# Output projection and second FFN product with the activations stationary and the weights streamed 512 wide

## The chip, the cores and the metric

The kernel runs on one core of a Trainium2 chip. The metric is the device time in microseconds; the median of three runs of the kernel before is 356.52 (356.47 to 356.79). PE is the matmul engine, ACT and DVE the two engines for elementwise work, SP the queue that issues the transfers.

## The reference, cut to what matters

One decoder block over 256 tokens of 1024 features, all in fp32. What the change touches is the end of the attention part and the FFN:

```
proj = einsum('bsd,de->bse', rms_norm(x, attn_norm_g), w_in)   # q, k, v, forget and gate logits
... two attention branches o_a, o_b of 512 features each ...
merged = gates[:, :, 0] * (o_a @ w_branch_moba) + gates[:, :, 1] * (o_b @ w_branch_fox)
x = x + einsum('bsd,de->bse', merged, w_out)                    # 1024 -> 1024
h2 = rms_norm(x, ffn_norm_g)
up = einsum('bsd,df->bsf', h2, w_ffn_up)                        # 1024 -> 2 * 2816
u, g = split(up, 2, axis=-1)
g = causal_depthwise_conv(g, ffn_conv_w, ffn_conv_b)            # 3 taps over the tokens
x = x + einsum('bsf,fd->bsd', silu(g) * u, w_ffn_down)          # 2816 -> 1024
```

## The kernel before

Every matrix product is made of fp32r matmuls on split operands: a value is the sum of a high part (rounded to fp32r by ACT) and a low part (the rest, by DVE). A product takes three terms: high x high, high x low, low x high.

**Weights.** They come in chunks of 1 MB in a fixed list (`chunks`: qkv, wg, wb, wo, then wu with wd between), over three raw buffers. Each chunk has two halves of 128 x 1024. `load` issues the transfer on SP and writes the split of a half: L125 on ACT makes `whi`, L126 on DVE makes `wlo`. There are six pairs of `whi`/`wlo` buffers (`HB`), and `use` asks for the splits five halves ahead (`AHEAD`). So a split waits until PE has read the half six places earlier.

**Layout.** The q/k/v projections (`project`, L236) hold a tile of 128 tokens stationary and stream 512 weight columns; their result is tokens by features. All products behind the attention hold 128 x 128 of weights stationary and stream 256 tokens; their result is features by tokens. So x1 (x plus the attention part, in place of `xT`), the FFN and the result stand features by tokens.

**Around the change.** `wb` (L527 to L529) makes `mh`, `ml`, the parts of merged. The output projection (L553 to L555) has four chunks: 0 and 1 cover the first half of the contraction, 2 and 3 the second. With chunks 2 and 3, each half finishes two blocks of 128 features: DVE adds the residual (L558), ACT and DVE make the parts of x1 times the norm's gain, `hx` (L562, L563; tag `pp`), and ACT squares (L564). The sums of squares go through a matmul with ones in `norm2` (L572), called in the middle of the second up tile, and become `rs2`, by which the FFN's products are scaled afterwards (L600). The first FFN product (`up_products`, L590 and L591) has 22 tiles; one matmul streams both parts of `hx` 512 wide, one the high part against the low weights. The second (`down`, L639 to L641) comes after every second up tile, in eleven steps, and accumulates into four PSUM banks; in the last step the result's blocks are finished one after another, each with an add (L619) and a store.

PE's order is written out by hand and is the program order. The order of ACT's and DVE's queues is made by a scheduler when the kernel is built; each engine works through its queue strictly in that order.

Of the kernel before, what the change touches and what calls it, by code (L numbers as in the profile page):

```python
# [8 lines left out]
F32 = mybir.dt.float32  # L9
# [32 lines left out]
def decoder_block(ctx, tc, a, out):  # L42
# [7 lines left out]
    def T(shape, tag, bufs=1, dt=F32):  # L50
        return sb.tile(shape, dt, tag=tag, bufs=bufs, name=tag)

    def bank():
        return ps.tile([P, 512], F32, tag="bank", bufs=8, name="bank")
# [395 lines left out]
    def banks():  # L450
        return [bank() for _ in range(NT)]
# [13 lines left out]
    project(2, pv, 1)  # L465
    finish_v(pv, 0)
    pq = banks()
    project(3, pq, 0)
    turn_qk(qn, kn, 0)
    project(3, pq, 1)  # L470
# [66 lines left out]


    hx = T([P, KT, 2, 2, P], "pp", 1, F32R)
    sq2 = T([P, 4, 2 * S], "V")  # L540
    acc = [bank() for _ in range(4)]
    x1 = xT
    sqs = T([P, S], "sqs")
    for c in range(4):
        for h in range(2):
            wh, wl = use(("wo", c), h)
            j = 2 * (c % 2) + h
            for i in range(2):
                o = acc[j][:, i * S:(i + 1) * S]
                for k4 in range(4):  # L550
                    k = 4 * (c // 2) + k4
                    w = slice(k4 * 256 + i * P, k4 * 256 + (i + 1) * P)
                    nc.tensor.matmul(o, wh[:, w], pairs(mh[:, k]), start=(k == 0 and i == 0), stop=False)  # L553
                    nc.tensor.matmul(o, wh[:, w], pairs(ml[:, k]), start=False, stop=False)  # L554
                    nc.tensor.matmul(o, wl[:, w], pairs(mh[:, k]), start=False, stop=(k == KT - 1 and i == 1))  # L555
            if c >= 2:
                xx = x1[:, 2 * j:2 * j + 2]
                nc.vector.tensor_tensor(halves(xx), apart(acc[j]), halves(xx), op=ALU.add)  # L558
                for b in (2 * j, 2 * j + 1):
                    g = col(C_G2 + b)  # L560
                    xb = x1[:, b].rearrange("p (a t) -> p a t", a=2)
                    nc.scalar.activation(hx[:, b, :, 0], xb, AF.Copy, scale=g)  # L562
                    nc.vector.scalar_tensor_tensor(hx[:, b, :, 1], xb, g, hx[:, b, :, 0].bitcast(F32), op0=ALU.mult, op1=ALU.subtract)  # L563
                nc.scalar.activation(sq2[:, j].rearrange("p (b t) -> p b t", b=2), xx, AF.Square)  # L564
    for dst, src in ((0, 1), (2, 3), (0, 2)):
        nc.vector.tensor_tensor(sq2[:, dst], sq2[:, dst], sq2[:, src], op=ALU.add)
    nc.vector.tensor_tensor(sqs, sq2[:, 0, 0:S], sq2[:, 0, S:2 * S], op=ALU.add)
    rs2 = T([P, S], "rs2")

    def norm2():  # L570
        sp = bank()
        nc.tensor.matmul(sp[:, 0:S], ones, sqs, start=True, stop=True)  # L572
        rsqrt_mean(rs2, sp[:, 0:S], D, [S], "pT", 4)


    acts = {}
# [1 line left out]
    def up_products(f):  # L578
        two = banks()
        for h in range(2):  # L580
            if f == 1 and h == 1:
                norm2()
            wh, wl = use(("wu", f), h)
            for i in range(2):
                for k4 in range(4):
                    k = 4 * h + k4
                    w = slice(k4 * 256 + i * P, k4 * 256 + (i + 1) * P)
                    both = hx[:, k].rearrange("p a l t -> p (l t) a")
                    high = hx[:, k, :, 0].rearrange("p a t -> p t a")
                    nc.tensor.matmul(two[i], wh[:, w], both, start=(k == 0), stop=False)  # L590
                    nc.tensor.matmul(two[i][:, 0:S], wl[:, w], high, start=False, stop=(k == KT - 1))  # L591
        return two

    def up_finish(f, two):
# [17 lines left out]
        nc.scalar.activation(ah, av, AF.Copy)  # L612
        nc.vector.tensor_tensor(al, av, ah.bitcast(F32), op=ALU.subtract)

    acc = []
    yy = lt[:, :, S:2 * S]

    def residual(dst, ps_, d, n):
        nc.vector.tensor_tensor(halves(dst), apart(ps_, n), halves(x1[:, d:d + n]), op=ALU.add)  # L619

    def down(p):
        if p == 0:
            acc[:] = [(b, c) for b in banks() + banks() for c in (0, S)]
        ac = acts.pop(p)
        last = p == NF // 2 - 1
        if last:
            acc[6:] = [(bank(), 0) for _ in range(2)]
        w2 = [use(("wd", p), h) for h in range(2)]
        order = [(h, d) for d in ((0, 1), (2, 3), (4, 5), (6,), (7,)) for h in range(2)] if last else [(h, (d,)) for h in range(2) for d in range(KT)]
        for h, ds in order:  # L630
            wh, wl = w2[h]
            ah, al = pairs(ac[:, h]), pairs(ac[:, 2 + h])
            for d in ds:
                bk, c = acc[d]
                o = bk[:, c:c + S]
                w = slice(d * P, (d + 1) * P)
                first = h == 0 and c == 0 and (p == 0 or last and d > 5)
                end = h == 1 and (d == ds[-1] if last else p == NF // 2 - 2 and d == KT - 1)
                nc.tensor.matmul(o, wh[:, w], ah, start=first, stop=False)  # L639
                nc.tensor.matmul(o, wh[:, w], al, start=False, stop=False)  # L640
                nc.tensor.matmul(o, wl[:, w], ah, start=False, stop=end)  # L641
            if last and h == 1:
                n = len(ds)
                y = yy[:, ds[0]:ds[0] + n]
                residual(y, acc[ds[0]][0][:, 0:n * S], ds[0], n)
                nc.sync.dma_start(out[:, ds[0]:ds[0] + n], y)
        if p == NF // 2 - 2:
            residual(x1[:, 6:8], acc[6][0], 6, 2)

    first = [up_products(f) for f in range(2)]  # L650
    for f in range(NF):
        up_finish(f, first[f] if f < 2 else up_products(f))
# [6 lines left out]
def _layout(i):  # L659
    f = np.float32  # L660
    x = i["x"][0]
    w = i["w_in"][0]
    k128 = lambda m: m.reshape(-1, P, m.shape[1]).transpose(1, 0, 2)
    c = np.ascontiguousarray
    a = {}
    w6 = w[:, :6 * W4].reshape(D, 6, W4 // 2, 2).transpose(0, 1, 3, 2).reshape(D, 6 * W4)
    qkv = w6.reshape(2, 4, P, 6, W4)
    a["qkv"] = c(qkv.transpose(3, 0, 2, 1, 4).reshape(6, 2, P, 2048)[1:])
    lead = np.concatenate([x.T.reshape(KT, P, S), w6[:, :W4].reshape(KT, P, W4)], 2)
    a["lead"] = c(lead)  # L670
    a["wf"] = c(k128(w[:, 6 * W4:6 * W4 + NH]))
    wg = w[:, 6 * W4 + NH:].reshape(KT, P, 2, KT, P)
    a["wg"] = c(wg.transpose(3, 1, 0, 2, 4).reshape(KT, P, 2048))
    wb = np.concatenate([i["w_branch_moba"][0], i["w_branch_fox"][0]]).reshape(KT, P, 4, 256)
    a["wb"] = c(wb.transpose(2, 1, 0, 3).reshape(4, P, 2048))
    wo = i["w_out"][0].reshape(2, 4, P, 2, 2, 256)
    a["wo"] = c(wo.transpose(0, 3, 2, 4, 1, 5).reshape(4, P, 2048))
    wu = i["w_ffn_up"][0].reshape(KT, P, 2, NF, P)
    a["wu"] = c(wu.transpose(3, 1, 0, 2, 4).reshape(NF, P, 2048))
    a["wd"] = c(i["w_ffn_down"][0].reshape(NF // 2, 2, P, D).transpose(0, 2, 1, 3).reshape(NF // 2, P, 2048))  # L680
    sm = np.empty((P, C_END), f)
    a["g1"] = c(i["attn_norm_g"][0].reshape(KT, P).T)
    sm[:, C_G2:C_G2 + 8] = i["ffn_norm_g"][0].reshape(KT, P).T
    sm[:, C_BG:C_BG + 16] = i["b_gate"][0].reshape(2 * KT, P).T
    sm[:, C_CW:C_CW + 66] = i["ffn_conv_w"][0].reshape(3 * NF, P).T
    sm[:, C_CB:C_CB + 22] = i["ffn_conv_b"][0].reshape(NF, P).T
    gm = ["moba_q_norm_g", "moba_k_norm_g", "fox_q_norm_g", "fox_k_norm_g"]
    for j, n in enumerate(gm):
        sm[0:64, C_QG + j] = sm[64:128, C_QG + j] = i[n][0]
        if j < 2:  # L690
            sm[0:16, C_QG + j] = sm[64:80, C_QG + j] = 1.0
            sm[:, C_GR + 16 * j:C_GR + 16 * (j + 1)] = i[n][0][None, 0:16]
    sm[:, C_BF:C_BF + 8] = i["b_forget"][0][None]
    a["smalls"] = sm
    cs = np.zeros((P, 832), f)
    cs[:, 0:128] = np.eye(P)
    tri = np.tril(np.ones((P, P), f))
    cs[:, 128:256] = tri.T
    cs[:, 256:384] = 1.0
    mask = np.where(tri > 0, f(0), f(BIG))  # L700
    cs[:, 384:512] = mask
    cs[:, 640:768] = mask
    inv = np.power(f(500000.0), -np.arange(HALF, dtype=f) * f(2.0) / f(16)).astype(f)
    ang = np.arange(S, dtype=f)[:, None] * inv[None]
    co, si = np.cos(ang), np.sin(ang)
    tab = np.concatenate([co, co, si, -si], 1).reshape(NT, P, 32).transpose(1, 0, 2)
    cs[:, 768:832] = tab.reshape(P, 64)
    a["consts"] = cs
    return a
# [15 lines left out]
```

## Time and profile before

| | |
|---|---|
| median of three runs | 356.52 us |
| profiled execution | 357.34 us, span 355.5 us |
| PE busy | 350.4 us, 99% |
| DVE busy | 285.5 us, 80% |
| ACT busy | 228.8 us, 64% |
| read from memory | 66.6 MB, 190 GB/s over the span |

Busy time of PE is modelled and says little; the distance between the starts of two matmuls says how fast the stream is. In the timeline a row has the start, the duration, engine, line, operation, output and inputs, stationary shape and streamed shape, and in brackets the idle time before it and what ended that. In the chain of waits a piece has its start, its length and what it was.

### The profile page before, as it was taken

Reading aid. Unit: us, or ns where it says so; the run is one execution under the profiler, and the core shown is the slowest. Engines: PE = TensorE matmul, PEld = TensorE weight load, DVE = VectorE, ACT = ScalarE, POOL = GpSimd, SP = SyncE. Lnnn points to the kernel's source line nnn. Section 1 sums busy time; section 2 is a strip of 40 time slices with the busy share of each in tenths; the row PEclk is TensorE's granted clock in tenths of the full one; section 3 lists DMA queues with packets and bytes.
Section 4 is the critical chain, followed back from the end, with each engine's and each line's share of the span. In section 5 each row is a group of like instructions: output and inputs, shape, how many; then the busy total and the mean of one; then the engine's idle time right before and its main releaser. Section 6 shows DMA issues by size and latency. Waiting matters only on the chain.

```text
span 355.5 us, 6596 instructions
## 1 busy us (share of the span) xinstructions
PE 350.4 (99%) x2620; PEld 324.3 (91%) x2620; DVE 285.5 (80%) x534; ACT 228.8 (64%) x406; POOL 0.4 (0%) x6
## 2 busy tenths in 40 slices
PE   8999999999999999999999999999999999999995
PEld 4888888889899999999999999999999999999995
DVE  4989969888867756994997998897878788797953
ACT  5967576678849873553878866665756656666620
POOL 0000000000000000000000000000000000000000
PEclk9999999999999999999999999999999999999999
DMA  7986663663624453545644358655645646554003
GB/s 259 410 336 237 221 255 130 227 237 120 238 92 147 133 225 118 202 166 227 229 144 187 153 165 295 211 193 206 236 162 194 238 166 205 223 189 167 2 0 118
DMA packets 12558, 68.07 MB, mean 191 GB/s; under 512 B 1512, under 2 KB 3696, under 8 KB 5104
## 3 DMA queue, kind: packets, MB, share of 16 engines
q1 hardware_dynamic: 11328, 66.60, 51.7%
q10 hardware_dynamic: 1200, 1.06, 1.0%
q8 instruction: 20, 0.33, 0.4%
q14 instruction: 10, 0.08, 0.1%
HBM read 66.60 MB, written 1.06 MB: 190 GB/s over the span
## 4 chain that ended last, share of the span: by engine, by line
PE 98%; ACT 1%; DVE 0%; issue 0%
PE bank L590 22%; PE bank L236 18%; PE bank L591 11%; PE bank L641 6%; PE bank L640 6%; PE bank L639 5%; PE bank L436 4%; PE bank L438 4%; PE bank L437 4%; PE bank L527 2%; PE bank L555 2%; PE bank L554 2%; PE bank L529 2%; PE bank L528 2%; PE bank L553 2%; PE bank L411 2%
## 5 line engine op out<-in xcount | busy, mean ns | idle before, releaser
L126 DVE TENSOR_TENSOR wlo<-raw,whi 128x1024 fp32r<-128x1024 f32 x118 | 144.0, 1222 | 38.2 <-ACT whi L125 37.2
L125 ACT ACTIVATE whi<-raw 128x1024 fp32r<-128x1024 f32 x118 | 123.7, 1054 | 66.5 <-PE bank L590 20.7
L590 PE MATMUL bank<-pp,whi 128*128 128x512 f32 x352 | 116.2, 383 | 0.0
L591 PE MATMUL bank<-pp,wlo 128*128 128x256 f32 x352 | 95.9, 273 | 0.0
L590 PEld LDWEIGHTS bank<-pp,whi 128*128 128x128 f32 x352 | 66.6, 189 | 9.2
L591 PEld LDWEIGHTS bank<-pp,wlo 128*128 128x128 f32 x352 | 67.6, 192 | 0.0
L436 PE MATMUL bank<-xh,whi 128*128 128x256 f32 x128 | 35.6, 278 | 0.1
L437 PE MATMUL bank<-xl,whi 128*128 128x256 f32 x128 | 35.2, 275 | 0.0
L438 PE MATMUL bank<-xh,wlo 128*128 128x256 f32 x128 | 35.2, 275 | 0.0
L639 PE MATMUL bank<-qT,whi 128*128 128x256 f32 x112 | 30.8, 275 | 0.0
L640 PE MATMUL bank<-qT,whi 128*128 128x256 f32 x112 | 30.8, 275 | 0.0
L641 PE MATMUL bank<-qT,wlo 128*128 128x256 f32 x112 | 30.8, 275 | 0.0
L236 PE MATMUL bank<-whi,xh 128*128 128x512 f32 x96 | 29.8, 393 | 0.0
L236 PE MATMUL bank<-wlo,xh 128*128 128x512 f32 x96 | 29.1, 385 | 0.0
L236 PE MATMUL bank<-whi,xl 128*128 128x512 f32 x96 | 28.7, 380 | 0.0
L436 PEld LDWEIGHTS bank<-xh,whi 128*128 128x128 f32 x128 | 24.6, 192 | 1.1 <-ACT qT L282 0.5
L438 PEld LDWEIGHTS bank<-xh,wlo 128*128 128x128 f32 x128 | 24.6, 192 | 0.0
L437 PEld LDWEIGHTS bank<-xl,whi 128*128 128x128 f32 x128 | 24.6, 192 | 0.0
L639 PEld LDWEIGHTS bank<-qT,whi 128*128 128x128 f32 x112 | 21.5, 192 | 0.2
L640 PEld LDWEIGHTS bank<-qT,whi 128*128 128x128 f32 x112 | 21.5, 192 | 0.0
L641 PEld LDWEIGHTS bank<-qT,wlo 128*128 128x128 f32 x112 | 21.5, 192 | 0.0
L236 PEld LDWEIGHTS bank<-wlo,xh 128*128 128x128 f32 x96 | 18.3, 192 | 3.1 <-DVE wlo L103 0.6
(158 smaller groups left out, 644.7 us busy)
## 6 DMA issues: line engine op xcount, KB each, us to landing
raw<-in_wu SPq DMA_DIRECT2D x22, 1024.0 KB, 4.8
raw<-in_wd SPq DMA_DIRECT2D x11, 1024.0 KB, 4.8
raw<-in_qkv SPq DMA_DIRECT2D x9, 1024.0 KB, 5.0
raw<-in_wg SPq DMA_DIRECT2D x8, 1024.0 KB, 4.9
raw<-in_wb SPq DMA_DIRECT2D x4, 1024.0 KB, 5.2
raw<-in_wo SPq DMA_DIRECT2D x4, 1024.0 KB, 4.8
lead<-in_lead SPq DMA_DIRECT2D x8, 384.0 KB, 6.6
raw<-in_qkv SPq DMA_DIRECT2D x2, 512.0 KB, 8.0
```

What stands on the lines that cost most here:

```text
L125: whi = nc.scalar.activation(hi, raw, AF.Copy)
L126: nc.vector.tensor_tensor(lo, raw, hi.bitcast(F32), op=ALU.subtract)
L236: nc.tensor.matmul(pt[t], lhs[:, k, t * P:(t + 1) * P], rhs, start=(k == 0 and i == 0), stop=(k == KT - 1 and i == 2))
L411: nc.tensor.matmul(op[o:o + HD, n * S + i * P:(n + 1) * S], V[:, i, vc:vc + HD], pT[:, j, c], start=(i == 0), stop=(i == 1))
L436: nc.tensor.matmul(o, wh[:, w], rh, start=(k == 0 and i == 0), stop=False)
L437: nc.tensor.matmul(o, wh[:, w], rl, start=False, stop=False)
L438: nc.tensor.matmul(o, wl[:, w], rh, start=False, stop=(k == KT - 1 and i == 1))
L590: nc.tensor.matmul(two[i], wh[:, w], both, start=(k == 0), stop=False)
L591: nc.tensor.matmul(two[i][:, 0:S], wl[:, w], high, start=False, stop=(k == KT - 1))
L639: nc.tensor.matmul(o, wh[:, w], ah, start=first, stop=False)
L640: nc.tensor.matmul(o, wh[:, w], al, start=False, stop=False)
L641: nc.tensor.matmul(o, wl[:, w], ah, start=False, stop=end)
```

## The change

The weights of the output projection and of the second FFN product are now streamed 512 columns at a time past stationary tiles of 128 x 128 activations, as in the q/k/v projections. x1 and the result become tokens by features. x is therefore loaded a second time, in that order (`xn`, 1 MB), over the place of `xT`. The output projection makes four tiles of 128 tokens x 512 features; each holds both halves of a weight chunk for both token tiles. The input of the first FFN product must still stand features by tokens, so x1 goes through 16 transposes on PE (`turn_x`), out of whose banks ACT and DVE make the parts of `hx` (`split_h`). The squares are summed by ACT along the features; `norm2` works on two columns and is called ahead of the first up tile, and `norm2_row` spreads its result by a matmul in the middle of the second up tile. Weights and result are rearranged on the host, outside the time.

```diff
+    x1 = xT
+    nc.sync.dma_start(x1, a["xn"])
     project(3, pq, 0)
...
-    for c in range(4):
-        for h in range(2):
-            wh, wl = use(("wo", c), h)
-            ...
-                    nc.tensor.matmul(o, wh[:, w], pairs(mh[:, k]), start=(k == 0 and i == 0), stop=False)
...
+    def wo(kh, dh, t, w2):
+        for h in range(2):
+            wh, wl = w2[h]
+            for k2 in range(2):
+                k = 4 * kh + 2 * h + k2
+                rh, rl = (pairs(w[:, k2 * 512:(k2 + 1) * 512]) for w in (wh, wl))
+                for i, (lhs, rhs) in enumerate(((mh, rh), (mh, rl), (ml, rh))):
+                    nc.tensor.matmul(acc[t][dh], lhs[:, k, t * P:(t + 1) * P], rhs, start=(k == 0 and i == 0), stop=(k == KT - 1 and i == 2))
+
+    def residual(t, dh):
+        xx = x1[:, place(t, dh)]
+        nc.vector.tensor_tensor(xx, wide(acc[t][dh]), xx, op=ALU.add)
+        nc.scalar.activation(T([P, 2, S], "sq", 2), xx, AF.Square, accum_out=ssq[:, t, dh:dh + 1])
+
+    def turn_x(dh, t):
+        for j in range(2):
+            if t == 0:
+                hb[dh, j] = bank()
+            for b in range(2):
+                c = b * S + t * P
+                nc.tensor.transpose(hb[dh, j][:, c:c + P], x1[:, 4 * t + 2 * dh + j, b * P:(b + 1) * P], ident)
+
+    def split_h(dh):
+        for j in range(2):
+            for b in range(2):
+                d = 4 * dh + 2 * j + b
+                src = hb[dh, j][:, b * S:(b + 1) * S].rearrange("p (a t) -> p a t", a=2)
+                g = col(C_G2 + d)
+                nc.scalar.activation(hx[:, d, :, 0], src, AF.Copy, scale=g)
+                nc.vector.scalar_tensor_tensor(hx[:, d, :, 1], src, g, hx[:, d, :, 0].bitcast(F32), op0=ALU.mult, op1=ALU.subtract)
+
+    for kh in range(2):
+        for dh in range(2):
+            w2 = [use(("wo", 2 * kh + dh), h) for h in range(2)]
+            for t in range(NT):
+                wo(kh, dh, t, w2)
+                if kh == 1:
+                    residual(t, dh)
+                if kh == 1 and dh == 1 and t == 0:
+                    for u in range(NT):
+                        turn_x(0, u)
+                    split_h(0)
+    turn_x(1, 0)
+
+    def last_turn():
+        turn_x(1, 1)
+        split_h(1)
...
+                if f == 0 and h == 0 and i == 0:
+                    last_turn()
...
+            for i, (lhs, rhs) in enumerate(((ah, rh), (ah, rl), (al, rh))):
+                nc.tensor.matmul(o, lhs, rhs, start=(first and i == 0), stop=(end and i == 2))
...
+            for h in range(2):
+                for dh in range(2):
+                    for t in range(NT):
+                        end = h == 1 and p == NF // 2 - 2 and t == dh == 1
+                        tile_of(h, t, dh, acc[t][dh], every, p == 0 and h == 0, end)
...
+    r2 = norm2()
     first = [up_products(f) for f in range(2)]
```

On ACT, at the seam between output projection and first up tile, the queue of the kernel before: `L562` makes a high part of `hx`, `L125` the split of a weight half, `L564` a square, `L598` belongs to the FFN.

```order
L562 ACTIVATE pp_1999<-lead_79,sm_80 128x2x128 x2
L564 ACTIVATE V_2000<-lead_79 128x512
L125 ACTIVATE whi_2269<-raw_2226 128x1024
L562 ACTIVATE pp_1999<-lead_79,sm_80 128x2x128 x2
L564 ACTIVATE V_2000<-lead_79 128x512
L125 ACTIVATE whi_2291<-raw_2289 128x1024
L598 ACTIVATE lows_2364<-bank_2267 128x256
L125 ACTIVATE whi_2313<-raw_2289 128x1024
L598 ACTIVATE lows_2364<-bank_2268 128x256
L125 ACTIVATE whi_2344<-raw_2342 128x1024
L190 ACT_TABLE_LOAD
```

The same place of ACT's queue now: `L580` makes a high part out of a bank of transposes (2140 holds blocks 0 and 1, 2143 blocks 2 and 3, 2173 blocks 4 and 5, 2176 blocks 6 and 7), `whi_2121` and `whi_2191` are the halves of chunk wu 2, `L564` the square of the last tile.

```order
L580 ACTIVATE pp_2000<-bank_2140,sm_80 128x2x128
L125 ACTIVATE whi_2121<-raw_2119 128x1024
L580 ACTIVATE pp_2000<-bank_2143,sm_80 128x2x128
L125 ACTIVATE whi_2191<-raw_2119 128x1024
L564 ACTIVATE sq_2171,ssq_2005<-lead_79 128x512
L580 ACTIVATE pp_2000<-bank_2173,sm_80 128x2x128
L580 ACTIVATE pp_2000<-bank_2176,sm_80 128x2x128
L580 ACTIVATE pp_2000<-bank_2173,sm_80 128x2x128
L190 ACT_TABLE_LOAD
L190 ACTIVATE rsv_2182<-rsv_2182 128x2
L580 ACTIVATE pp_2000<-bank_2176,sm_80 128x2x128
L191 ACT_TABLE_LOAD
```

Two splits now stand among the high parts, and the table load of the norm, which stood behind the first FFN evacuations, stands ahead of the high part of block 7; the second high part out of a bank waits for DVE's low part of the first.

On DVE, the end of the seam before: `L558` is a residual, `L563` a low part of `hx`, `L126` the low half of a weight split, `L566` an add of squares.

```order
L558 TENSOR_TENSOR lead_79<-bank_2003,lead_79 128x2x256
L126 TENSOR_TENSOR wlo_2229<-raw_2226,whi_2228 128x1024
L563 SCALAR_TENSOR_TENSOR pp_1999<-lead_79,sm_80,pp_1999 128x2x128 x2
L558 TENSOR_TENSOR lead_79<-bank_2004,lead_79 128x2x256
L126 TENSOR_TENSOR wlo_2270<-raw_2226,whi_2269 128x1024
L563 SCALAR_TENSOR_TENSOR pp_1999<-lead_79,sm_80,pp_1999 128x2x128 x2
L566 TENSOR_TENSOR V_2000<-V_2000 128x512 x2
```

And now: `L563` is a residual, `L581` a low part out of the same banks, `L603` the add of the sums of squares.

```order
L563 TENSOR_TENSOR lead_79<-bank_2002,lead_79 128x2x256
L581 SCALAR_TENSOR_TENSOR pp_2000<-bank_2140,sm_80,pp_2000 128x2x128
L581 SCALAR_TENSOR_TENSOR pp_2000<-bank_2143,sm_80,pp_2000 128x2x128
L581 SCALAR_TENSOR_TENSOR pp_2000<-bank_2140,sm_80,pp_2000 128x2x128
L126 TENSOR_TENSOR wlo_2122<-raw_2119,whi_2121 128x1024
L581 SCALAR_TENSOR_TENSOR pp_2000<-bank_2143,sm_80,pp_2000 128x2x128
L563 TENSOR_TENSOR lead_79<-bank_2004,lead_79 128x2x256
L126 TENSOR_TENSOR wlo_2192<-raw_2119,whi_2191 128x1024
L603 TENSOR_TENSOR ss2_2179<-ssq_2005 128x2
L581 SCALAR_TENSOR_TENSOR pp_2000<-bank_2173,sm_80,pp_2000 128x2x128
```

A weight split moved ahead of the low part of block 3 and of the last residual, another ahead of the low part of block 4.

## Rows read from the trace of the kernel before

**Rows 1.** The page: PE's busy time, and its granted clock in 40 slices.
```profile
PE 350.4 (99%) x2620; PEld 324.3 (91%) x2620; DVE 285.5 (80%) x534; ACT 228.8 (64%) x406; POOL 0.4 (0%) x6
...
PEclk9999999999999999999999999999999999999999
```

**Rows 2.** The page: the chain of waits by engine.
```profile
PE 98%; ACT 1%; DVE 0%; issue 0%
```

**Rows 3.** Timeline of PE: start and duration in us, 256-wide matmuls, and what follows.
```profile
155.33 0.28 PE L553 MATMUL bank<-xh,whi 128*128 128x256 f32 x1
...
176.77 0.38 PE L590 MATMUL bank<-pp,whi 128*128 128x512 f32 x1
...
340.84 0.28 PE L639 MATMUL bank<-qT,whi 128*128 128x256 f32 x1
...
346.20 0.28 PE L639 MATMUL bank<-kT,whi 128*128 128x256 f32 x1
```

**Rows 4.** Timeline of PE: first and twenty-first of a run of 512-wide matmuls.
```profile
40.72 0.59 PE L236 MATMUL bank<-wlo,xh 128*128 128x512 f32 x2
...
45.03 0.38 PE L236 MATMUL bank<-whi,xl 128*128 128x512 f32 x1
```

**Rows 5.** Chain of waits at the seam: start, length in us, what.
```profile
180.21 0.27 PE bank L590
...
180.59 0.29 PE bank L590
```

**Rows 6.** Chain of waits: fp32 passes of 128 (L423, L345) and 256 columns.
```profile
27.47 0.44 PE bank L423 x4
...
58.00 0.22 PE bank L345 x2
...
184.92 0.43 PE bank L572 x2
```

**Rows 7.** Timeline of ACT, output projection to second up tile.
```profile
166.20 1.06 ACT L125 ACTIVATE whi<-raw 128x1024 fp32r<-128x1024 f32 x1 [1.63 <-PE bank L554]
...
173.43 0.61 ACT L564 ACTIVATE V<-lead 128x512 f32<-128x512 f32 x1
...
185.97 1.28 ACT L190 ACT_TABLE_LOAD   x1
187.26 0.42 ACT L190 ACTIVATE pT<-pT 128x256 f32<-128x256 f32 x1
```

**Rows 8.** Timeline of DVE at the seam.
```profile
175.80 1.21 DVE L126 TENSOR_TENSOR wlo<-raw,whi 128x1024 fp32r<-128x1024 f32 x1
176.93 0.87 DVE L563 SCALAR_TENSOR_TENSOR pp<-lead,sm,pp 128x256 fp32r<-128x256 f32 x2
177.72 0.68 DVE L558 TENSOR_TENSOR lead<-bank,lead 128x512 f32<-128x512 f32 x1
```

**Rows 9.** Groups by line and form, whole span: busy us, mean ns | idle.
```profile
L598 ACT ACTIVATE lows<-bank 128x256 f32<-128x256 f32 x44 | 16.3, 371 | 2.1 <-PE bank L591 2.1
...
L382 ACT ACTIVATION_READ_ACCUMULATOR s<-s,nm 128x1 f32 x32 | 6.2, 192 | 0.0
...
L562 ACT ACTIVATE pp<-lead,sm 128x256 fp32r<-128x256 f32 x8 | 3.6, 500 | 0.8 <-DVE lead L558 0.6
...
L563 DVE SCALAR_TENSOR_TENSOR pp<-lead,sm,pp 128x256 fp32r<-128x256 f32 x8 | 3.5, 479 | 0.0
...
L558 DVE TENSOR_TENSOR lead<-bank,lead 128x512 f32<-128x512 f32 x4 | 2.7, 685 | 0.4 <-PE bank L555 0.4
```

**Rows 10.** Transfers of the page (us to landing); ACT's weight splits, 30 to 45 us.
```profile
raw<-in_qkv SPq DMA_DIRECT2D x9, 1024.0 KB, 5.0
...
L125 ACT ACTIVATE whi<-raw 128x1024 fp32r<-128x1024 f32 x7 | 7.2, 1051 | 2.7 <-PE bank L236 2.7
```

**Rows 11.** Chain of waits: its last piece.
```profile
351.76 0.42 DVE lead L619
```

More of the change, by code (lines that the diff above doesn't have):

```diff
@@ L539, in decoder_block @@
     hx = T([P, KT, 2, 2, P], "pp", 1, F32R)
[L540 to L543, printed above, removed]
-    for c in range(4):
-        for h in range(2):
-            wh, wl = use(("wo", c), h)
[L547 to L552, printed above, removed]
-                    nc.tensor.matmul(o, wh[:, w], pairs(mh[:, k]), start=(k == 0 and i == 0), stop=False)
[L554 to L568, printed above, removed]
-    def norm2():
-        sp = bank()
-        nc.tensor.matmul(sp[:, 0:S], ones, sqs, start=True, stop=True)
-        rsqrt_mean(rs2, sp[:, 0:S], D, [S], "pT", 4)
+    acc = [[bank() for _ in range(2)] for _ in range(NT)]
+    ssq = T([P, NT, 2], "ssq")
+    rs2 = T([P, S], "rsB")
@@ new lines, in place, with wide @@
+    def place(t, dh):
+        return slice(4 * t + 2 * dh, 4 * t + 2 * dh + 2)
+    def wide(ps_):
+        return ps_.rearrange("p (j c) -> p j c", j=2)
+    def wo(kh, dh, t, w2):
+        for h in range(2):
+            wh, wl = w2[h]
[4 more added lines that the diff above has]
+                    nc.tensor.matmul(acc[t][dh], lhs[:, k, t * P:(t + 1) * P], rhs, start=(k == 0 and i == 0), stop=(k == KT - 1 and i == 2))
@@ new lines, in split_h @@
+    def split_h(dh):
[6 more added lines that the diff above has]
+                nc.vector.scalar_tensor_tensor(hx[:, d, :, 1], src, g, hx[:, d, :, 0].bitcast(F32), op0=ALU.mult, op1=ALU.subtract)
+    hb = {}
+    for kh in range(2):
[9 more added lines that the diff above has]
+                    split_h(0)
@@ new lines, in decoder_block, with norm2_row @@
+    turn_x(1, 0)
+    def last_turn():
+        turn_x(1, 1)
+        split_h(1)
+    def norm2():
+        ss = T([P, NT], "ss2")
+        nc.vector.tensor_tensor(ss, ssq[:, :, 0], ssq[:, :, 1], op=ALU.add)
+        r2 = T([P, NT], "r2")
+        rsqrt_mean(r2, ss, D, [NT], "rsv")
+        return r2
+    def norm2_row(r2):
+        rp = bank()
+        for t in range(NT):
+            nc.tensor.matmul(rp[:, t * P:(t + 1) * P], r2[:, t:t + 1].to_broadcast([P, P]), ident, start=True, stop=True)
+        nc.vector.tensor_copy(rs2, rp[:, 0:S])
@@ L581, in up_products @@
             if f == 1 and h == 1:
-                norm2()
+                norm2_row(r2)
             wh, wl = use(("wu", f), h)
@@ L613, in up_finish @@
         nc.vector.tensor_tensor(al, av, ah.bitcast(F32), op=ALU.subtract)
-    acc = []
     yy = lt[:, :, S:2 * S]
-    def residual(dst, ps_, d, n):
-        nc.vector.tensor_tensor(halves(dst), apart(ps_, n), halves(x1[:, d:d + n]), op=ALU.add)
     def down(p):
         if p == 0:
-            acc[:] = [(b, c) for b in banks() + banks() for c in (0, S)]
+            acc[:] = [banks() for _ in range(NT)]
         ac = acts.pop(p)
         last = p == NF // 2 - 1
-        if last:
-            acc[6:] = [(bank(), 0) for _ in range(2)]
@@ L628, in down, with tile_of @@
         w2 = [use(("wd", p), h) for h in range(2)]
-        order = [(h, d) for d in ((0, 1), (2, 3), (4, 5), (6,), (7,)) for h in range(2)] if last else [(h, (d,)) for h in range(2) for d in range(KT)]
-        for h, ds in order:
+        def tile_of(h, t, dh, o, cut, first, end):
             wh, wl = w2[h]
[L632 to L646, printed above, removed]
@@ L647, in down @@
-        if p == NF // 2 - 2:
-            residual(x1[:, 6:8], acc[6][0], 6, 2)
+            rh, rl = (pairs(w[:, dh * 512:(dh + 1) * 512])[:, cut] for w in (wh, wl))
+            ah, al = (ac[:, n, t * P:(t + 1) * P] for n in (h, 2 + h))
+            for i, (lhs, rhs) in enumerate(((ah, rh), (ah, rl), (al, rh))):
+                nc.tensor.matmul(o, lhs, rhs, start=(first and i == 0), stop=(end and i == 2))
+        every = slice(0, S)
+        if not last:
+            for h in range(2):
+                for dh in range(2):
+                    for t in range(NT):
+                        end = h == 1 and p == NF // 2 - 2 and t == dh == 1
+                        tile_of(h, t, dh, acc[t][dh], every, p == 0 and h == 0, end)
+            if p == NF // 2 - 2:
+                xx = x1[:, place(1, 1)]
+                nc.vector.tensor_tensor(xx, wide(acc[1][1]), xx, op=ALU.add)
+            return
@@ new lines, in down @@
+        for dh, t in ((0, 0), (0, 1), (1, 0)):
+            for h in range(2):
+                tile_of(h, t, dh, acc[t][dh], every, False, h == 1)
+            at = place(t, dh)
+            nc.vector.tensor_tensor(yy[:, at], wide(acc[t][dh]), x1[:, at], op=ALU.add)
+            nc.sync.dma_start(out[:, at], yy[:, at])
+        for j in range(2):
+            o = bank()[:, 0:S]
+            for h in range(2):
+                tile_of(h, 1, 1, o, slice(j * P, (j + 1) * P), h == 0, h == 1)
+            at = 6 + j
+            nc.vector.tensor_tensor(yy[:, at], o, x1[:, at], op=ALU.add)
+            nc.sync.dma_start(out[:, at], yy[:, at])
@@ L675, in _layout @@
     a["wb"] = c(wb.transpose(2, 1, 0, 3).reshape(4, P, 2048))
-    wo = i["w_out"][0].reshape(2, 4, P, 2, 2, 256)
-    a["wo"] = c(wo.transpose(0, 3, 2, 4, 1, 5).reshape(4, P, 2048))
+    twos = lambda m: m.reshape(m.shape[0], -1, 256, 2).transpose(0, 1, 3, 2).reshape(m.shape)
+    wo = twos(i["w_out"][0]).reshape(2, 4, P, 2, 512)
+    a["wo"] = c(wo.transpose(0, 3, 2, 1, 4).reshape(4, P, 2048))
+    a["xn"] = c(x.reshape(NT, P, 4, S).transpose(1, 0, 2, 3).reshape(P, KT, S))
     wu = i["w_ffn_up"][0].reshape(KT, P, 2, NF, P)
     a["wu"] = c(wu.transpose(3, 1, 0, 2, 4).reshape(NF, P, 2048))
-    a["wd"] = c(i["w_ffn_down"][0].reshape(NF // 2, 2, P, D).transpose(0, 2, 1, 3).reshape(NF // 2, P, 2048))
+    a["wd"] = c(twos(i["w_ffn_down"][0]).reshape(NF // 2, 2, P, D).transpose(0, 2, 1, 3).reshape(NF // 2, P, 2048))
     sm = np.empty((P, C_END), f)
@@ L723 @@
     r = run_bass_kernel_spmd(nc, [{"in_" + n: v for n, v in arrays.items()}], core_ids=[0])
-    return np.ascontiguousarray(r.results[0]["out_0"].transpose(2, 1, 0)).reshape(1, S, D)
+    return np.ascontiguousarray(r.results[0]["out_0"].reshape(P, NT, D).transpose(1, 0, 2)).reshape(1, S, D)
```

## The prediction

> **What bounds the kernel now.** I read the page's busy times and slices first: TensorE (PE) is busy for 99% of the span at full granted clock, 2.4 GHz [rows 1]. Then the chain of waits: 98% of it is PE [rows 2]. So the kernel is one stream of matmuls, and a change is worth what it does to the distance between two matmul starts, plus every place where PE stands still. The starts in the timeline give the distances. A 256-wide fp32r matmul takes (176.77 - 155.33) / 192 = 111.7 ns in the output projection, and (346.20 - 340.84) / 48 = 111.7 ns in one step of the second FFN product [rows 3]. A 512-wide one in the q/k/v projections, which have the form that the change introduces (activations stationary, weights streamed), takes (45.03 - 40.72) / 20 = 215.5 ns [rows 4], not 223. The one place where data came late near the change is the seam between output projection and first FFN product: two pieces of 0.27 and 0.29 us where one takes 0.216, together 0.12 us [rows 5].
>
> **The stream.** The output projection has 4 chunks of 2 halves with 24 matmuls: 192 x 0.1117 = 21.44 us. Afterwards it has 2 x 2 x 2 tiles of 12 wide matmuls: 96 x 0.2155 = 20.69, a gain of 0.75. The second FFN product has 11 x 48 = 528 narrow matmuls, 58.96 us (8 column blocks x 3 x 2 halves in each step). Afterwards ten steps have 24 wide ones, the last has 18 wide and 12 narrow: 258 x 0.2155 + 12 x 0.1117 = 56.94, a gain of 2.02. Together -2.77. The ends for this term: 216.5 instead of 215.5 ns would cost 0.35; nothing in the rows supports more.
>
> TensorE: Matmul & The Clock Gate of the Trainium skill (Back-to-back issue gap) gives columns / 2.4 plus 2.5 ns for a warm matmul. That fits the wide row (215.8), but makes a narrow one 109.2, and by it the stream would gain 720 x 0.1092 - 354 x 0.2158 - 12 x 0.1092 = 0.9 us only, and the forecast would be 1.9 us higher. The trace has 111.7 in both places, so the rows decide.
>
> **The transposes.** h2's input now goes through PE: 2 halves x 2 token tiles x 4 = 16 fp32 transposes of 128 x 128. The trace has two fp32 transposes that stream 128 columns, 0.22 us for both, and four fp32 passes over 128 columns in 0.44 [rows 6], so 0.111 each: 16 x 0.111 = +1.78, all on the path. Low end: 0.056 each, were they as fast per column as fp32r (+0.9); high end: a restart of 0.1 us at each of the three groups (+2.1). I take 1.78. The norm's matmul stays equal: two fp32 passes of 256 columns, 0.43 [rows 6], become four of 128, 0.44, under the same waits as before.
>
> **The seam, step by step.** Here the order of ACT's and DVE's queues decides. I count from the first output-projection matmul as 0. PE finishes token tile 0 of the last chunk at 84 x 0.2155 = 18.10, eight transposes at 18.99, tile 1 at 21.58, four transposes at 22.02, and then wants h2's blocks k = 0, 1, 2, 3, one per 0.327 us. The last four transposes stand after those, and blocks 4 to 7 are wanted after another four pairs.
>
> Prices: a weight split is 1.06 on ACT, 1.21 on DVE (the next starts 1.13 later) [rows 7, 8]; a residual add 0.68, a low part 0.48 (spacing 0.40) [rows 8, 9]; a high part out of PSUM, which no row has with this output, lies between 0.37 (from PSUM, L598) and 0.50 (to the same tile, L562), taken as 0.41, the next starting 0.33 later as L563's follow each other 0.08 before the end [rows 9]; a square of 512 columns 0.61 [rows 7] plus 0.19 for reading its sum [rows 9]; a table load 1.28 [rows 7].
>
> (1) ACT's split of the first half of chunk wu 2 stands between two high parts. It reuses the buffer of wo 3's first half, which PE now reads twice, for tile 0 and tile 1, so it comes free at 18.99 + 6 x 0.2155 and about 0.2 for the drain, 20.5. Such waits for PE exist already: 1.63 us before the split at 166.20 [rows 7]. ACT splits from 20.7 to 21.8, DVE from 21.8 to 23.0, and only then comes the low part of block 3, ready at 23.4. PE wants it at 22.02 + 3 x 0.327 = 23.0: a stall of 0.4.
>
> (2) Behind that in DVE's queue stands the residual of tile 1's second half, which could start at 21.8 and now runs from 23.35 to 24.05. The last transposes wait for it; PE is there at 23.75: 0.3, and about 0.1 more, since x1 is their stationary operand and its load cannot run ahead.
>
> (3) DVE then splits wu 2's second half (to 25.2) and waits for the last square (24.1 to 24.9 on ACT) before the low part of block 4, ready at 25.7, in time. The high part of block 5 waits for the low part of block 4, which reads the same PSUM bank; block 5 is ready at 26.7. PE wants it at 26.1: 0.55.
>
> (4) Between the high parts of blocks 5 and 7 stand a table load and the Ln of the norm. Load 26.1 to 27.4, Ln, high part 27.5 to 27.9, low part to 28.4. PE wants block 7 at 27.35: 1.1.
>
> Stalls 0.4 + 0.4 + 0.55 + 1.1 = 2.45, against 0.12 before. The same walk over the queues of the kernel before gives 0.09 where its trace shows 0.12, so I trust it to some 0.5 us; the two bounds of the high part move the sum by -0.25 and +0.5.
>
> ScalarE: Activation LUTs of the Trainium skill (What ACT_TABLE_LOAD costs) adds a drain of about 1.38 us to each load. In the trace the next activation starts 10 ns after the load's end [rows 7], so the sum has no drain; by the page it would be 1.4 higher, which is one of the rivals.
>
> **What costs nothing.** x in token order is one more megabyte on SP's queue, behind the sixth of the nine undivided q/k/v weight loads; such a megabyte lands in 5.0 us [rows 10], and nothing in the queue waits for this one. ACT's splits between 30 and 45 us waited for PE, 2.7 us in all, and never for a transfer [rows 10], and they run five halves ahead of their use (five times some 2.6 us). Cover gone, a late weight would stop PE by at most a transfer, 5 us. The adds of squares that DVE loses were off the path. After the seam r2 is ready at about 29.9 and its broadcast matmul comes at 32.7. Six hi/lo buffers leave some 9 us before the next late split is used. The tail keeps its form: the last block is again six narrow matmuls, an add of 0.42 [rows 11] and a store of the same size.
>
> **Sum.** -2.77 + 1.78 + 2.45 - 0.12 + 0.01 = +1.35. The profiled execution took 357.34 (span 355.5), so 358.7 there; the median of the runs is 356.52, and 357.9 is my forecast in its terms.
>
> **Rivals.** *Seam hidden* (faster): the high and low parts come in time, stalls at most 0.3, -0.8, 355.7. For it: the seam before hid nearly everything with as many splits in the queues. Against: it needs block 7 by 26.1, although its high part stands behind a table load, behind a square, behind a residual that starts 1.8 us late. It decides from a sum of stalls under 1.1 us. *Load beside activations* (no change): the table load does not hold up block 7. Then stall (4) goes and about 1.35 remains: +0.25, 356.8. Against it: 187.26 follows 185.97 + 1.28 [rows 7]. *Drain* (slower): with 1.38 us of drain before the load, stall (4) is 2.5, +2.7, 359.2; the page named above says so, the row does not. *Late weights* from the extra megabyte: up to +5 once; the rows of slack speak against. *No narrower gain*: the wide form at 223 ns, twice the narrow one, would gain nothing, +4.1, 360.6; rows 4 exclude nearly all of it.
>
> **Numbers.** Forecast 70% (own range 357.3 to 358.7), seam hidden 12%, load beside activations 10%, drain 5%, late weights or lost gain 3%. Low end 356.3, between the no-change case and the hidden seam, high end 359.3: this leaves out the hidden seam and the top 3%. About 0.2% (0.7 us) is what a measurement of this kernel can tell from no change. Faster by more: 0.12. Within: 0.13 (the 10%, and the forecast's low edge). Slower: 0.75.
>
> **What would show it.** Starts 215.5 ns apart in both changed products, 16 transposes of 0.11. In the seam: pieces of the chain over 0.3 us at blocks 3, 5 and 7 of the first FFN tile and before the last transposes; a DVE residual that starts 1.8 us after the projection's last product; a table load between two high parts. Wrong would be a seam with under 1 us of gaps, gaps outside it, or a distance over 217 ns.

## The result and the profile after

The changed kernel takes 358.50 us (median of 6 runs, 357.88 to 358.77) against 356.53 for the kernel before in the same rounds (6 runs, 356.47 to 356.79). The ratio is 1.0051, 95% interval 1.0038 to 1.0064: slower by 2.0 us, inside the forecast range, 0.6 above the forecast time.

The profiled execution took 358.07, span 356.3. The page, PE's busy time, the chain of waits by engine, and the group of the wide up products:

```profile
PE 349.5 (98%) x2284; PEld 313.5 (88%) x2284; DVE 284.1 (80%) x532; ACT 228.8 (64%) x410; POOL 0.4 (0%) x6
...
PE 95%; ACT 2%; DVE 1%; issue 0%
...
L629 PE MATMUL bank<-pp,whi 128*128 128x512 f32 x352 | 116.6, 383 | 1.7 <-DVE pp L581 1.7
```

PE's share of the chain falls from 98% [rows 2] to 95%, and the first FFN product waits 1.7 us for low parts (L581). The group shows idle time only once a matmul's modelled end has passed. To size a stall, compare starts in the timeline of PE instead (start and duration, then engine, line, operation, tiles and shapes):

```profile
154.45 0.38 PE L559 MATMUL bank<-whi,xh 128*128 128x512 f32 x1
...
172.59 1.04 PE L572 MATMUL bank<-cst,lead 128*128 128x128 f32 x8
173.38 0.46 PE L559 MATMUL bank<-whi,xh 128*128 128x512 f32 x1
...
176.05 0.60 PE L572 MATMUL bank<-cst,lead 128*128 128x128 f32 x4
176.41 0.46 PE L629 MATMUL bank<-pp,whi 128*128 128x512 f32 x1
176.71 0.27 PE L630 MATMUL bank<-pp,wlo 128*128 128x256 f32 x1
...
177.36 0.27 PE L630 MATMUL bank<-pp,wlo 128*128 128x256 f32 x1
177.91 0.48 PE L629 MATMUL bank<-pp,whi 128*128 128x512 f32 x1 [0.28 <-DVE pp L581]
178.23 0.27 PE L630 MATMUL bank<-pp,wlo 128*128 128x256 f32 x1
178.51 0.66 PE L572 MATMUL bank<-cst,lead 128*128 128x128 f32 x4
178.92 0.46 PE L629 MATMUL bank<-pp,whi 128*128 128x512 f32 x1
179.22 0.27 PE L630 MATMUL bank<-pp,wlo 128*128 128x256 f32 x1
...
180.53 0.27 PE L630 MATMUL bank<-pp,wlo 128*128 128x256 f32 x1
181.23 0.48 PE L629 MATMUL bank<-pp,whi 128*128 128x512 f32 x1 [0.43 <-DVE pp L581]
181.55 0.27 PE L630 MATMUL bank<-pp,wlo 128*128 128x256 f32 x1
...
181.88 0.27 PE L630 MATMUL bank<-pp,wlo 128*128 128x256 f32 x1
183.11 0.48 PE L629 MATMUL bank<-pp,whi 128*128 128x512 f32 x1 [0.96 <-DVE pp L581]
183.43 0.27 PE L630 MATMUL bank<-pp,wlo 128*128 128x256 f32 x1
...
206.26 0.38 PE L670 MATMUL bank<-whi,qT 128*128 128x512 f32 x1
...
211.44 0.38 PE L629 MATMUL bank<-pp,whi 128*128 128x512 f32 x1
...
352.25 0.28 PE L670 MATMUL bank<-whi,kT 128*128 128x256 f32 x1
```

A narrow product (L630) is normally followed 0.11 us later. After 177.36 the next starts 0.55 later (block 3), after 178.23 0.28 (the last transposes), after 180.53 0.70 (block 5), after 181.88 1.23 (block 7): 0.44 + 0.17 + 0.59 + 1.12 = 2.32 us of waiting. After each of the three waits for a block, the second matmul also comes late: 177.91 to 178.23 is 0.32, where 0.22 is normal. That adds 3 x 0.10. The four last transposes, which follow a wait too, take 0.05 more than the four at 176.05 (178.51 to 179.22 is 0.71, 176.05 to 176.71 is 0.66). In all the seam costs 2.67 us.

The chain of waits through it (start, length in us, what) names what held each block:

```profile
175.26 0.95 ACT whi L125
...
176.23 0.40 DVE wlo L126
...
177.38 0.48 DVE pp L581
177.85 0.60 DVE lead L563
178.45 1.13 DVE wlo L126
...
179.67 0.49 DVE pp L581
...
180.19 0.47 ACT pp L580
...
180.68 1.28 ACT L190
...
181.97 0.20 ACT rsv L190
182.17 0.37 ACT pp L580
...
182.57 0.49 DVE pp L581
```

Read from above: weight split on ACT and DVE, low part of block 3 (177.38), last residual (177.85), the next weight split, low part of block 4 (179.67), high part of block 5 (180.19), table load, Ln, high part of block 7 (182.17) and its low part. The longest piece in front of block 7 is the load of 1.28.

One difference of the two traces is not the change's. The first output-projection matmul starts at 155.33 in the trace of before [rows 3] and at 154.45 here, though of the change only the load of x in token order comes earlier. In the seven experiments below it starts between 154.31 and 154.80, whichever kernel they were made from, so the profiled run of before merely reached it late. I therefore compare from the first output-projection matmul to the last matmul of all, which the timeline of PE before has at 351.45:

```profile
351.45 0.28 PE L641 MATMUL bank<-kT,wlo 128*128 128x256 f32 x1
```

Before, 155.33 to 351.45 is 196.12 us; after, 154.45 to 352.25 is 197.80 us: +1.67 (from the unrounded starts).

### The profile page after: what moved, and what is told of

It reads as the page before. It is cut to its first block, busy times and chain, and to the rows that moved or that the text cites. A ratio compares the mean times of both kernels' runs of the same rounds, so it can differ in the third digit from the quotient of the medians.

```text
span 356.3 us, 5923 instructions
## 1 busy us (share of the span) xinstructions
PE 349.5 (98%) x2284; PEld 313.5 (88%) x2284; DVE 284.1 (80%) x532; ACT 228.8 (64%) x410; POOL 0.4 (0%) x6
## 4 chain that ended last, share of the span: by engine, by line
PE 95%; ACT 2%; DVE 1%; issue 0%
PE bank L629 21%; PE bank L236 18%; PE bank L670 16%; PE bank L630 10%; PE bank L559 5%; PE bank L436 4%; PE bank L437 4%; PE bank L438 4%; PE bank L529 2%; PE bank L531 2%; PE bank L530 2%; PE bank L411 2%; PE bank L374 1%; PE bank L157 1%; PE bank L398 1%; ACT whi L125 1%
## 5 line engine op out<-in xcount | busy, mean ns | idle before, releaser
L126 DVE TENSOR_TENSOR wlo<-raw,whi 128x1024 fp32r<-128x1024 f32 x118 | 144.0, 1222 | 41.0 <-ACT whi L125 39.6
L125 ACT ACTIVATE whi<-raw 128x1024 fp32r<-128x1024 f32 x118 | 123.9, 1055 | 69.4 <-PE bank L629 25.7
L630 PE MATMUL bank<-pp,wlo 128*128 128x256 f32 x352 | 96.0, 273 | 0.0
L630 PEld LDWEIGHTS bank<-pp,wlo 128*128 128x128 f32 x352 | 67.5, 192 | 0.2
L670 PE MATMUL bank<-whi,qT 128*128 128x512 f32 x112 | 34.5, 379 | 0.0
L670 PEld LDWEIGHTS bank<-whi,qT 128*128 128x128 f32 x112 | 21.2, 189 | 3.0
L670 PE MATMUL bank<-wlo,qT 128*128 128x512 f32 x56 | 21.2, 379 | 0.0
L236 PEld LDWEIGHTS bank<-whi,xh 128*128 128x128 f32 x96 | 17.7, 192 | 3.4 <-ACT whi L102 0.8
L236 PEld LDWEIGHTS bank<-whi,xl 128*128 128x128 f32 x96 | 18.1, 189 | 2.6
L670 PE MATMUL bank<-whi,kT 128*128 128x512 f32 (+1 forms) x68 | 19.8, 367 | 0.0
```

Source lines behind the costliest of these rows:

```text
L125: whi = nc.scalar.activation(hi, raw, AF.Copy)
L126: nc.vector.tensor_tensor(lo, raw, hi.bitcast(F32), op=ALU.subtract)
L236: nc.tensor.matmul(pt[t], lhs[:, k, t * P:(t + 1) * P], rhs, start=(k == 0 and i == 0), stop=(k == KT - 1 and i == 2))
L670: nc.tensor.matmul(o, lhs, rhs, start=(first and i == 0), stop=(end and i == 2))
```

## Experiments

My theory: the stream gains 2.7, the transposes cost 1.8, and four waits at the seam, each by the order of ACT's, DVE's or PE's queue, cost 2.3 to 2.7. Its rival: the loss lies in transposes and stream, and the seam is only where it shows. All runs have five rounds beside the kernel before. Its median was 356.69 beside the first two experiments, the second FFN product alone and the sixteen transposes, and 356.66 beside the other three. "Stretch" is the time from first output-projection matmul to last matmul.

**Load and weight split behind the last high part.**

```diff
-        nc.scalar.activation(t, v, AF.Ln)
+        ln = nc.scalar.activation(t, v, AF.Ln)
+        if behind:                      # high part of block 7
+            after(ln, behind[0])
...
+            if len(behind) == 1:        # the next weight split
+                after(whi, behind[0])
...
-                norm2_row(r2)           # ahead of f 1, second half
+        if f == 1:
+            norm2_row(r2[0])            # behind f 1
```

> The changed kernel with another order on ScalarE alone: the high parts of all four blocks of h's second half stand in one row, and the weight split and the norm's two table loads stand behind them; the norm's broadcast matmul moves from before the last half of FFN tile 1 to behind it. TensorE's stream of products is the same. Seam theory: the load between the high parts of blocks 5 and 7 holds TensorE for 1.12 us and a restart of 0.10 before block 7; both go, the other three stalls stay: 358.5 - 1.2 = 357.3 us. Rival (the wait is shown at block 7, but the low parts on VectorE or the weight split are late anyway, so another instruction takes the load's place): 358.5, or at most 0.3 below. Rival (the loss is not in the seam but in transposes and stream): 358.5.

Measured 356.88 (11 runs, 356.68 to 357.49), ratio 1.0014 [1.0005, 1.0023]; stretch 196.57, 1.22 under the changed kernel. In its timeline ACT has the high parts in one row, and the load behind them:

```profile
179.05 0.82 ACT L586 ACTIVATE pp<-bank,sm 128x256 fp32r<-128x256 f32 x2
180.06 0.87 ACT L586 ACTIVATE pp<-bank,sm 128x256 fp32r<-128x256 f32 x2 [0.19 <-DVE pp L587]
180.83 1.05 ACT L126 ACTIVATE whi<-raw 128x1024 fp32r<-128x1024 f32 x1
181.89 1.28 ACT L194 ACT_TABLE_LOAD   x1
```

The gap before block 7 is gone, and the first three stalls stay at 0.44, 0.17 and 0.59. The edit also moves the norm's steps and its matmul behind the blocks, but of what stood ahead of block 7's high part on ACT in the changed kernel only the load and the Ln are gone. The load's place was worth 1.22 us (1.12 of waiting and 0.10 for the late second matmul), as theory (1.2) had it. The median fell by 1.6, the ratio by 0.0037, 1.3 us.

**The other stalls: PE's own order.** In addition to the edit before:

```diff
+        up_half(0, 0, ta, by_block)
+        last_turn()
+        r2.append(norm2())
+        up_half(1, 0, tb, by_tile)
+        up_half(0, 1, ta, by_block)
+        up_half(1, 1, tb, by_tile)
+        norm2_row(r2[0])
```

> As the run before, and in addition TensorE's own order at the seam changes: FFN tile 0's first half goes block by block over both column halves (block 3 is wanted 1 us later), the last four transposes stand behind it, and FFN tile 1's first half (2.6 us of products that need blocks 0 to 3 only) stands before blocks 4 to 7 are wanted. No instruction of TensorE is added or removed. Seam theory: all four stalls go, 2.3 us of waiting and 0.3 to 0.4 of restarts: 358.5 - 2.7 = 355.8, which is 0.7 under the kernel before (356.5), close to what stream and transposes alone give (-2.7 + 1.8 = -0.9: 355.6). Rival (the transposes cost more than 0.11 each, or the stream gained less, so that the loss lies outside the seam): over 357. Rival (the late splits of wu 2 and 3 that now stand behind the blocks stop TensorE later): 356.5 to 358.5, with gaps at FFN tiles 2 and 3.

Measured 357.39 (11 runs, 357.07 to 357.84), ratio 1.0021 [1.0012, 1.0029], stretch 196.82: not the 355.8 that I expected. All four stalls are gone from its trace, but a new one stands at the norm's matmul. The chain of waits there:

```profile
187.36 0.23 PE bank L633
...
187.64 0.15 DVE rsv L199
187.79 1.15 DVE wlo L130
...
189.16 0.68 PE bank L618 x4
```

and the timeline of DVE ahead of it:

```profile
185.55 0.16 DVE L198 SCALAR_TENSOR_TENSOR rsv<-rsv 128x2 f32<-128x2 f32 x1 [0.29 <-ACT rsv L197]
186.49 1.23 DVE L130 TENSOR_TENSOR wlo<-raw,whi 128x1024 fp32r<-128x1024 f32 x1 [0.78 <-ACT whi L126]
187.64 0.15 DVE L199 TENSOR_TENSOR rsv<-rsv 128x2 f32<-128x2 f32 x1
187.71 1.23 DVE L130 TENSOR_TENSOR wlo<-raw,whi 128x1024 fp32r<-128x1024 f32 x1
188.85 0.15 DVE L200 SCALAR_TENSOR_TENSOR r<-rsv 128x2 f32<-128x2 f32 x1
```

L198 to L200 are the norm's last steps, 0.15 us each, and between them stand two weight splits of 1.23. PE, no longer held up at the blocks, reaches the norm's matmul at 187.5 and waits 1.63 us. None of the expected outcomes named this. By its time alone the run would fit both rivals; the late splits come nearest, but the gap stands at the norm's matmul behind FFN tile 1, not at tiles 2 and 3. The time says neither that the seam theory fails nor that it holds, so the next run removes this wait.

**The norm's matmul half a tile later.**

```diff
         up_half(1, 1, tb, by_tile)
+        tc2 = banks()
+        up_half(2, 0, tc2, by_tile)
         norm2_row(r2[0])
+        up_half(2, 1, tc2, by_tile)
```

> As e2_blocks_late, and the norm's broadcast matmul moves on by one more half: it stands in the middle of FFN tile 2 instead of behind tile 1. In e2_blocks_late the four stalls at the blocks are gone from the trace, and TensorE waits once, 1.63 us, at that matmul, because the last three small steps of the norm stand behind weight splits of 1.2 us each in VectorE's queue (the last one ends at 189.0 us, the matmul was wanted at 187.5). Seam theory: in its new place it is wanted at 190.1, after the norm is ready; the wait and its restart of 0.07 go: 357.4 - 1.7 = 355.7. Rival (VectorE as a whole is behind at the seam, and the wait moves to FFN tiles 2 to 4, whose results then come late for the second FFN product): 357.4, with a new gap behind 190 us.

Measured 355.76 (8 runs, 355.24 to 355.97), ratio 0.9974 [0.9964, 0.9985]: faster than the kernel before. The stretch is 195.11, 2.69 under the changed kernel, and no start from the projection to the end is over 0.08 us late. The chain of waits from 176 to 192 us, by line, holds PE alone:

```profile
by line: PE bank L633 61.5%; PE bank L634 30.0%; PE bank L578 5.5%; PE bank L618 2.8%; PE bank L565 1.4%
```

So the seam's 2.67 us were order alone. The same instructions in other places take it to nothing. What is left, 195.11 against 196.12, is -1.01: about -0.9 from stream and transposes together, and -0.12 from the stalls that the seam of the kernel before had [rows 5].

**The second FFN product alone, on the kernel before.**

```diff
-                o = bk[:, c:c + S]
-                nc.tensor.matmul(o, wh[:, w], ah, start=first, stop=False)
...
+            for i, (lhs, rhs) in enumerate(((ah, rh), (ah, rl), (al, rh))):
+                nc.tensor.matmul(o, lhs, rhs, ...)
```

> The kernel before with the second FFN product alone turned to 512-wide streams past stationary activations (the output projection, the residual and the seam are as before; x1 and the weights keep their old arrangement, so the residual is added in the wrong places and the values differ, the work does not). My term: 258 wide and 12 narrow for 528 narrow, 258 x 0.2155 + 12 x 0.1117 - 528 x 0.1117 = -2.0: 356.5 - 2.0 = 354.5. Rival (a narrow matmul is 109.2 ns, as columns / 2.4 plus 2.5 ns would have it, and the 111.7 were stalls of weights that come late): about -0.7, 355.8. Rival (no gain, the wide form at twice the narrow one's distance): 356.5.

Measured 354.82 (5 runs, 354.33 to 354.91), ratio 0.9949 [0.9936, 0.9963]; stretch 194.18, a gain of 1.94 where my term was 2.02. In its timeline of PE a step of 24 wide matmuls takes 207.86 - 202.68 = 5.18 us, 215.8 ns each:

```profile
202.68 0.38 PE L636 MATMUL bank<-whi,qT 128*128 128x512 f32 x1
...
207.86 0.38 PE L590 MATMUL bank<-pp,whi 128*128 128x512 f32 x1
```

The rival with 109.2 ns for a narrow one expected 0.7 and falls. TensorE: Matmul & The Clock Gate of the Trainium skill (Back-to-back issue gap) gives columns / 2.4 plus 2.5 ns for a matmul by itself, and not for a stream of weight loads and matmuls, to which the prediction applied it. The wide distance of this stream agrees with it (215.8), the narrow one in both changed products does not (111.7 against 109.2).

**Sixteen more transposes.**

```diff
+        if f == 2:
+            spare = bank()
+            for n in range(16):
+                nc.tensor.transpose(spare[...], x1[...], ident)
```

> The changed kernel with 16 more fp32 transposes of 128 x 128 into a spare bank, in one piece in the dense stretch of the FFN, read by nobody. My term: 16 x 0.111 = +1.78, 360.3 (0.1 more if the first restarts). Rival (half price, as fast per column as fp32r): +0.9, 359.4. Rival (they are dearer than their pieces show, by weights that cannot load ahead): +2.4 or more, 360.9. If they hid in gaps: 358.5.

Measured 360.05 (4 runs, 359.78 to 360.54), ratio 1.0100 [1.0086, 1.0114]; stretch 199.54, +1.74. The timeline of PE:

```profile
196.01 1.91 PE L704 MATMUL bank<-cst,lead 128*128 128x128 f32 x16
197.67 0.46 PE L629 MATMUL bank<-pp,whi 128*128 128x512 f32 x1
197.97 0.27 PE L630 MATMUL bank<-pp,wlo 128*128 128x256 f32 x1
```

196.01 to 197.67 is 1.66, and the next distance is 0.30 instead of 0.22: 1.74 in all, 0.109 each. This extra 0.08 behind each group belongs to the group's price: counted in, four (176.05 to 176.71 above, less 0.22), eight (172.59 to 173.38, plus 0.08) and sixteen transposes all come to 0.109 or 0.110 each; only the four behind a wait come to 0.12. Half price, dearer and hidden in gaps all fall.

**Without x in token order.**

```diff
-    nc.sync.dma_start(x1, a["xn"])
```

> The changed kernel without the load of x in token order (1 MB on SP's queue): x1 starts from x in its features-by-tokens form, which is in the chip's memory anyway, so the residual's values differ and the work does not. My term: the megabyte costs nothing, 358.5 within 0.4. Rival (it delays the weights behind it, or the stretch at the program's start): 357.5 or less, with a gap that closes before 60 us.

Measured 358.18 (5 runs, 358.12 to 358.81), ratio 1.0047 [1.0035, 1.0060], which overlaps the changed kernel's interval; stretch 197.79 against 197.80, first output-projection matmul at 154.48 against 154.45. The megabyte costs nothing that can be seen.

**The gain without the transposes.** Only the second FFN product's -1.94 is a large gain, and it needs x1 as tokens by features only at the end, some 160 us after the seam. So the output projection and the seam stay as before, and x1 is turned off PE:

```diff
+    def turn(k):
+        nc.vector.transpose(turned[:, k:k + 2]..., x1[:, k:k + 2])
...
+                        yield yy[32 * q:32 * q + 32, 4 * t:4 * t + 4, d:d + 32], turned[32 * b:32 * b + 32, e::2, c:c + 32]
...
+                nc.sync.dma_start(*m)
```

> The kernel before with the second FFN product wide, as e3_down_only, but complete: x1 stays features by tokens for the output projection and the seam, VectorE turns it in blocks of 32 x 32 during FFN tiles 4 to 7 (four instructions of 512 columns), and 64 small transfers on SP's queue put the blocks in their places during tiles 8 to 20, so that the result is tokens by features without a transpose on TensorE. If the four instructions and the transfers stay beside the products: as e3_down_only, 354.8, the fastest so far. Rival (64 transfers of pieces of 128 bytes share queue and engines with the weights, and delay them): 355.5 or more, with gaps between 240 and 320 us. Rival (VectorE, 80% busy, falls behind): gaps just behind tiles 4 to 7.

Measured 354.79 (5 runs, 354.42 to 355.07), ratio 0.9946 [0.9934, 0.9959]: the fastest complete version, 1.9 us under the kernel before and 3.7 under the change. The stretch is 194.19, the same as with the second product alone. The group of VectorE's four instructions by line (busy us, mean ns, idle before):

```profile
L620 DVE STREAM_TRANSPOSE xh<-lead 128x512 f32<-128x512 f32 x4 | 2.7, 694 | 0.0
```

and the transfers in the list of DMA issues (KB each, median us to landing):

```profile
lead<-xh SPq DMA_DIRECT2D x64, 16.0 KB, 4.0
```

Both stay beside the products: PE's starts show no gap behind FFN tile 4 or between 240 and 320 us, where the two rivals put them. The price is 10,728 packets under 512 bytes instead of the 1,512 of the kernel before, which nothing waits for.

## Why the prediction was right

The direction and the mechanism held: a stream that gains less than the transposes and four waits at the seam cost. The terms, by the traces from first output-projection matmul to the last matmul:

| term | forecast | measured |
|---|---|---|
| **Stream**, output projection | -0.75 | 154.45 to 176.41, plus 0.08, less 12 x 0.109: 20.73, against 21.44: -0.71 |
| **Stream**, second FFN product | -2.02 | -1.94 |
| **Transposes** | +1.78 | +1.74 (16 x 0.109) |
| **Seam**, stalls less the 0.12 of before | +2.33 | 2.67 - 0.12 = +2.55 |
| **Sum**, with 0.01 forecast for the norm's matmul | +1.35 | +1.64 by terms, +1.67 by the stretch |

**Stream.** The wide distance is 215.8 to 216 ns, not 215.5: (172.59 - 154.45) / 84 = 216.0 in the output projection, (211.44 - 206.26) / 24 = 215.8 in a step of the second FFN product. Over 354 wide matmuls that is the missing 0.1.

**Seam (1)** foresaw the low part of block 3 at 23.4 us after the projection's start. The trace has 177.38 + 0.48 - 154.45 = 23.41, and the wait 0.44 for 0.4. One link of (1) does not show: the weight split was to wait for PE to free its buffer, at 20.5, and to start at 20.7. In the timelines of ACT and DVE the split and the residual of (2) are

```profile
175.14 1.06 ACT L125 ACTIVATE whi<-raw 128x1024 fp32r<-128x1024 f32 x1
...
177.77 0.68 DVE L563 TENSOR_TENSOR lead<-bank,lead 128x512 f32<-128x512 f32 x1
```

The split starts at 20.69, but ACT has no idle time before it: it follows the high parts ahead of it, so its place in the queue set its start, and the buffer did not hold it up. **(2)** foresaw the residual at 23.35; it starts at 23.32. But PE waits only 0.17 for it, not 0.3, since PE comes there at 178.34 (23.89) instead of 23.75, mostly by the late second matmul before. The restart of 0.1, which no row of before showed, came to 0.05; and the forecast's sum counted it on top, although a later PE would have waited less in (3). **(3)** 0.59 for 0.55. **(4)** 1.12 for 1.1, and the experiment on the load confirms its cause. What the step left out is the late second matmul after each wait for a block, 0.10 three times. So the seam's sum was 0.2 too small, although each of its parts was right to 0.2: the shorter wait of (2) hid a part of what was left out.

**Zero cost** held for x in token order, by its experiment, and for the tail: from the last matmul to the end of the span it is 4.05 us in both traces (351.45 to 355.5, 352.25 to 356.3). The medians leave 0.3 us between +1.97 and the stretch's +1.67, which is within the interval of the ratio (+1.4 to +2.3); no trace shows where they lie.

**Rivals.** *Seam hidden* and *Load beside activations* are ruled out by the trace and by the first experiment; the first became true only in the reordered kernel, at 355.76, where its price had been 355.7. *Drain* is ruled out on both sides of the load: it starts at 180.68, 0.02 after the high part ahead of it ends (180.19 + 0.47), and ACT's next activation starts at 181.97, 10 ns after 180.68 + 1.28, as in [rows 7]. ScalarE: Activation LUTs of the Trainium skill (What ACT_TABLE_LOAD costs) has another 1.38 for a drain; the load itself agrees (1.28), the drain does not show. *Late weights* and *No narrower gain* are ruled out by the runs without x in token order and with the second product alone.

## What to carry to other kernels

On this stream, 98% of it one engine, the gain of the cheaper form was small (2.7 of 356 us) and came within 0.1 us of its forecast. What decided was which instructions the new layout put between a producer and its first consumer, and a walk through the two queues with measured durations got these waits right to a few tenths. Where waits come from order, move the consumers that need nothing new ahead of those that wait, and move long background work (weight splits, table loads) behind the short steps on the path; then look again, since the next short step can stand behind the same work. And ask where the new layout is really needed: here the second FFN product brought most of the gain, and its transpose could be done by an engine with time to spare.

## What was not expected of the hardware

After a wait for a block, the distance from the first wide matmul to the next one is 0.32 us instead of 0.22, three times in the changed kernel and twice in the run with the load moved; after the wait before the transposes the four of them take 0.05 us more than four without a wait. Why it comes was not tried.

A matmul's width alone does not set the distance to the next one: in the first FFN product of the kernel before, where wide and narrow ones alternate, a narrow one is followed after 109 ns and a wide one after 218 (medians of 352 each), while narrow ones in a row are 111.7 apart and wide ones in a row 215.5 to 216.0.

The program's first 155 us varied by up to 1.0 us between executions (first output-projection matmul at 154.31 to 155.33 in nine profiles; 154.49, 154.80 and 155.33 in the three that are made from the kernel before and unchanged up to there). That is as much as half of the effect that was measured here, so two traces should be lined up at the first changed instruction.
